# Three stacked blocks instead of four in the differential scores, and new durations and order tables for the plan

## The chip, the cores and the metric

The kernel runs on one core of a Trainium2 chip. The metric is the device time of one execution in microseconds. Engines are named as in the profile: PE is TensorE (PEld its weight loads), DVE is VectorE, ACT is ScalarE, POOL is GpSimd, SP is SyncE, which here issues all the DMAs.

## The reference

Two layers of a diffusion block work on 512 image tokens and 256 context tokens, each of width 1024. In a layer one wide product makes the inputs of four mixers (a state space scan, differential attention, grouped-query attention, latent attention), their outputs go through `w_out`, and a squared-ReLU feed-forward part of width 4096 follows. In the last layer the context gives keys and values only. Everything is float32. The mixer that the change touches is this one, with four heads, score dimension 32 and value dimension 64:

```python
def differential_attention(q1, q2, k1, k2, v, lam, scale):
    p = attn_probs(q1, k1, scale) - lam * attn_probs(q2, k2, scale)
    return jnp.einsum('bkgqt,bktd->bkgqd', p.astype(v.dtype), v)
```

So each head takes two softmaxes, each over scores that contract 32 values.

## The kernel before

**Tiling.** Tokens lie along the free axis: a tile has 128 feature rows and up to 768 tokens (512 image, 256 context). Large products run on TensorE in its fast float32 format (fp32r). For precision each operand is split into a high and a low part, and three products are summed: high by high, high by low, low by high. The feed-forward part of a layer is nothing but such products; they carry the name `p` in the profile.

**Stages.** The span goes through: start-up with the modulation vectors and the first projections; the mixers of layer 0 up to about 450 us; its output projection and feed-forward part up to about 1035 us; the seam of the layers and the mixers of layer 1 up to about 1395 us; its output projection and feed-forward part; the final norm.

**The differential scores.** `diff_prep` (line 1164) applies the rotary embedding to a tile of queries or keys (four score vectors of 32 rows), splits it into a high tile and a low tile (`hldq`, `hldk`, ending in h and l), and builds four stacks from them, one for each of the two heads hh and the two softmaxes m. A stack is a tile of 128 rows: four blocks of 32 rows, each copied out of the high or the low tile by a DMA of its own from SBUF to SBUF, issued on SP's queue (`stack`, line 1160). The key stack `sdk` holds high, high, low, low, the query stack `sdq` high, low, high, low. One matmul that contracts the 128 rows thus sums all four products. `diff_attn` (line 1251) calls `scores` (line 1182) on these stacks; the result is `d_s` in the profile (512 and 256 columns for image queries). DVE takes its maximum (`d_m`), ACT the exponential (`d_p`), TensorE transposes the mix of the two softmaxes (`d_t`) and multiplies by the values (`d_o`), and DVE or ACT stores (`yo`). Two such pairs of heads, j = 0 and 1, are worked on in each of the two layers. The latent attention contracts 96 rows in three separate matmuls instead (`m_s`).

**The order of the work.** No engine takes its work in the order of the program text. Each call through `nc` is recorded as an operation of a `Plan` (class at line 168), and at the end `order` (line 387) plays a model of the five queues: an operation gets a duration from `cost` (line 322), a `late` time that its result needs on top, and a `HOP` between engines; SP's operations also occupy a DMA model with 330 GB/s. Where several operations of an engine could start, the one with the lowest rank goes first: its number in the program text plus an entry of the table `BIAS`, looked up by stage, engine and tile name; EARLY brings forward those that read PSUM. A second table, `ASK`, shifts the rank in which tiles of one kind get their buffers. Neighbouring matmuls on one output are one operation up to a duration of `GROUP`. The order that comes out is written into the five instruction lists, and each engine works through its list strictly in that order: an instruction that waits holds up everything behind it. All of this happens when the program is built; on the chip the plan has no instruction. Because every call is issued in one place, every instruction has line 474 in the profile, and tiles have to be told by name.

The entry of the cost function for a DMA was one line, whatever its two ends:

```python
        self.bytes = 4 * (x.box[1] - x.box[0]) * x.width()
        return 0.45, 1.4
```

and a DVE operation that the model starts while POOL is still busy (`pool > s`) was lengthened by `0.3 * min(cost, pool - s)`.

Of the kernel before, what the change touches and what calls it, by code (L numbers as in the profile page):

```python
# [13 lines left out]
F32R = mybir.dt.float32r  # L14
# [153 lines left out]
class Plan:  # L168
# [3 lines left out]
    HOP = 0.2  # L172
# [4 lines left out]
        (0, 'ACT', 'an'): -300, (0, 'ACT', 'cden'): 90, (0, 'ACT', 'ls'): -50, (0, 'ACT', 'n__q'): 570, (0, 'ACT', 'sq_'): -185, (0, 'ACT', 'wdks'):  # L177
        335, (0, 'ACT', 'wdqs'): -510, (0, 'ACT', 'xn_h'): -350, (0, 'DVE', 'an'): -50, (0, 'DVE', 'cden'): 125, (0, 'DVE', 'dg'): -140, (0, 'DVE',
        'ds'): -285, (0, 'DVE', 'gq'): -190, (0, 'DVE', 'gs_'): 295, (0, 'DVE', 'lpr'): 55, (0, 'DVE', 'ls'): -50, (0, 'DVE', 'modT'): -300, (0,
        'DVE', 'n__q'): -70, (0, 'DVE', 'n__r'): -120, (0, 'DVE', 'n__t'): 185, (0, 'DVE', 'neg'): 270, (0, 'DVE', 'sel'): -165, (0, 'DVE', 'sil'):  # L180
        340, (0, 'DVE', 'sq_'): 125, (0, 'PE', 'n__ms'): 210, (0, 'PE', 'pdk'): 180, (0, 'PE', 'pdq'): 300, (0, 'PE', 'pdv'): -5, (0, 'PE', 'pm'):
        -100, (0, 'PE', 'pn'): -5, (0, 'POOL', 'epsT'): 260, (0, 'POOL', 'heads'): -310, (0, 'POOL', 'tri'): -630, (0, 'POOL', 'wdks'): 390, (0,
        'POOL', 'wdqs'): -120, (0, 'SP', 'h_'): -5, (0, 'SP', 'par'): -15, (0, 'SP', 'rope'): -5, (0, 'SP', 'wdq_'): 245, (1, 'ACT', 'cd_'): 300, (1,
        'ACT', 'ckv'): 65, (1, 'ACT', 'cq'): 50, (1, 'ACT', 'cqh_h'): -315, (1, 'ACT', 'cqn_s'): 735, (1, 'ACT', 'cqx'): -180, (1, 'ACT', 'cvb'): 540,
# [8 lines left out]
        -440, (1, 'ACT', 'tdv'): -300, (1, 'ACT', 'tgvv'): 395, (1, 'ACT', 'wckvs'): -15, (1, 'ACT', 'wcqs'): -20, (1, 'ACT', 'wcqxs'): -70, (1,
        'ACT', 'wdvs'): 70, (1, 'ACT', 'wgas'): 710, (1, 'ACT', 'wgbs'): -275, (1, 'ACT', 'wgks'): -250, (1, 'ACT', 'wgvvs'): 5, (1, 'ACT', 'wks'):
        -290, (1, 'ACT', 'wst'): -600, (1, 'ACT', 'wus_'): 15, (1, 'ACT', 'wxss'): -120, (1, 'ACT', 'wzs'): 15, (1, 'ACT', 'yg_'): -635, (1, 'ACT',
        'yn_q'): 5, (1, 'ACT', 'yn_r'): 150, (1, 'ACT', 'yn_s'): -370, (1, 'ACT', 'ztz_'): -80, (1, 'DVE', 'acs'): -400, (1, 'DVE', 'btm'): -250, (1,
        'DVE', 'cd_'): -460, (1, 'DVE', 'ckv'): -705, (1, 'DVE', 'cq'): -135, (1, 'DVE', 'cqh_l'): -25, (1, 'DVE', 'cqn_q'): -440, (1, 'DVE',
        'cqn_r'): 615, (1, 'DVE', 'cqx'): -135, (1, 'DVE', 'cvb'): -650, (1, 'DVE', 'cvc'): -120, (1, 'DVE', 'cvxs'): -170, (1, 'DVE', 'd_____m'): 75,
# [23 lines left out]
        (2, 'ACT', 'acc_'): 275, (2, 'ACT', 'n___q'): -1015, (2, 'ACT', 'n___r'): 70, (2, 'ACT', 'r___'): -370, (2, 'ACT', 'sq___'): -255, (2, 'ACT',  # L222
# [99 lines left out]
    def cost(self, eng, name, args, kw, out):  # L322
# [3 lines left out]
        if eng == "PE":  # L326
# [1666 lines left out]
```

## Time and profile before

| | |
|---|---|
| time, three runs | 1800.88, 1803.46, 1809.90 us; median 1803.46 us |
| time of the profiled execution | 1804.01 us |
| its span, first to last instruction | 1802.3 us |
| mean granted TensorE clock | 0.985 of full speed |
| DMA issues | stack copies `sdk`, `sdq` of 96 or 64 KB, beside 256 KB weight tiles |

The profile shows one execution. Busy times are sums over an engine's instructions; an idle time is put down to what released the instruction after it. A row of a timeline gives start, duration, engine, operation, output tile and inputs, and how many neighbouring instructions it stands for; in square brackets is the idle time before it and what ended it. SPq is the queue of SP. The recorded duration of a matmul includes its way through the array, so neighbouring ones overlap.

### The profile page before, as it was taken

The page shows a single profiled execution, that of the slowest core. Times are in us where ns is not written, and L with a number is a line of the kernel's source. Part 1 is how long each engine was busy: PE and PEld are TensorE (multiplying, and loading weights), DVE is VectorE, ACT ScalarE, POOL GpSimd, SP SyncE. Part 2 cuts the span into 40 slices and gives each one's busy share as a digit, 9 for nine tenths or more (in the row PEclk, how much of TensorE's full clock was granted, in tenths as well). Part 3 has the DMA queues.
Part 4 walks back from the last instruction along what each step waited for, and adds up shares of the span by engine and source line. Part 5 has one row for each costly group of instructions (what it writes and reads, how often), then busy time and mean ns, then how long its engine had stood idle before and what let it go on. Part 6 is the DMA issues. An engine that isn't in the chain of part 4 may idle for free.

```text
span 1802.3 us, 30217 instructions
## 1 busy us (share of the span) xinstructions
PE 1736.5 (96%) x11246; PEld 1460.8 (81%) x11246; DVE 1099.7 (61%) x2092; ACT 880.8 (49%) x1791; POOL 473.8 (26%) x441
## 2 busy tenths in 40 slices
PE   7999999999999999999999998999899999999996
PEld 4777887678889888888888877787678998888886
DVE  5567868876576764534534286696987863333335
ACT  4356778777455123123123455676877752323243
POOL 2412341210334001001003773244311320101066
PEclk9989999989999999999999999999999999999999
DMA  9475422132454532532433434414015553233234
GB/s 350 118 196 145 125 77 70 47 108 85 141 157 141 164 129 94 160 111 93 162 112 99 146 103 114 104 46 112 20 41 165 175 172 94 94 95 97 95 114 127
DMA packets 116755, 216.29 MB, mean 120 GB/s; under 512 B 15360, under 2 KB 22528, under 8 KB 116608
## 3 DMA queue, kind: packets, MB, share of 16 engines
q1 hardware_dynamic: 116608, 214.36, 38.7%
q8 instruction: 89, 1.46, 0.3%
q14 instruction: 58, 0.48, 0.1%
HBM read 185.99 MB, written 8.13 MB: 108 GB/s over the span
## 4 chain that ended last, share of the span: by engine, by line
PE 82%; DVE 5%; DMA 3%; issue 3%; POOL 2%; ACT 2%; SPq 2%; DVEq 0%; POOLq 0%; ACTq 0%
PE p L474 47%; PE po L474 3%; PE pr L474 2%; PE m_s L474 2%; SPq L474 2%; PE pxs L474 2%; PE pz L474 2%; PE d_s L474 1%; PE m_o L474 1%; PE m_t L474 1%; PE d_o L474 1%; PE g_s L474 1%; PE g_o L474 1%; PE pe L474 1%; PE d_t L474 1%
## 5 line engine op out<-in xcount | busy, mean ns | idle before, releaser
L474 ACT ACTIVATE w_0s<-w 128x512 fp32r<-128x512 f32 x256 | 161.0, 629 | 383.4 <-PE p L474 364.0
L474 POOL TENSOR_TENSOR r<-r 128x512 f32<-128x512 f32 (+2 forms) x80 | 89.4, 1118 | 622.9 <-ACT a_0h L474 382.9
L474 DVE TENSOR_TENSOR w_0s<-w,w_0s 128x512 fp32r<-128x512 f32 x216 | 150.6, 698 | 166.0 <-ACT w_0s L474 165.7
L474 DVE SCALAR_TENSOR_TENSOR h<-p,modT,h 128x512 f32<-128x512 f32 (+1 forms) x104 | 63.0, 625 | 140.6 <-PE p L474 140.5
L474 DVE SCALAR_TENSOR_TENSOR junk<-mv,cb 128x512 bf16<-128x512 f32 x128 | 93.6, 741 | 66.5 <-DMA mv<-in_modw_dram 66.2
L474 ACT ACTIVATE r<-p 128x512 f32<-128x512 f32 (+2 forms) x80 | 47.9, 598 | 169.4 <-PE p L474 169.2
L474 DVE TENSOR_REDUCE d_m<-d_s 128x1 f32<-128x768 f32 (+1 forms) x80 | 66.9, 846 | 42.9 <-PE d_s L474 42.6
L474 ACT ACTIVATE d_p<-d_s,d_m 128x768 f32<-128x768 f32 (+1 forms) x80 | 65.0, 814 | 26.3 <-DVE d_m L474 18.3
L474 POOL TENSOR_TENSOR w_0s<-w,w_0s 128x512 fp32r<-128x512 f32 x40 | 53.7, 1352 | 47.5 <-ACT w_0s L474 41.4
L474 POOL TENSOR_TENSOR acc<-acc,sq 128x256 f32<-128x256 f32 (+1 forms) x48 | 50.9, 1061 | 39.3 <-ACT sq L474 29.6
L474 PE MATMUL p<-xm_0h,w_0s 128*128 128x512 f32 (+1 forms) x176 | 54.2, 354 | 0.1
L474 PE MATMUL p<-xm_3h,w_0s 128*128 128x512 f32 (+1 forms) x176 | 54.1, 353 | 0.0
L474 PE MATMUL p<-xm_1h,w_0s 128*128 128x512 f32 (+1 forms) x176 | 54.0, 353 | 0.0
L474 PE MATMUL p<-xm_7h,w_0s 128*128 128x512 f32 (+1 forms) x176 | 54.0, 354 | 0.0
L474 PE MATMUL p<-a_5h,w_0s 128*128 128x512 f32 (+1 forms) x176 | 54.0, 353 | 0.0
L474 PE MATMUL p<-a_2h,w_0s 128*128 128x512 f32 (+1 forms) x176 | 54.0, 353 | 0.0
L474 PE MATMUL p<-a_0h,w_0s 128*128 128x512 f32 (+1 forms) x176 | 54.0, 353 | 0.0
L474 PE MATMUL p<-a_4h,w_0s 128*128 128x512 f32 (+1 forms) x176 | 54.0, 353 | 0.0
L474 PE MATMUL p<-a_3h,w_0s 128*128 128x512 f32 (+1 forms) x176 | 53.9, 352 | 0.0
L474 PE MATMUL p<-xm_6h,w_0s 128*128 128x512 f32 (+1 forms) x176 | 53.9, 353 | 0.0
L474 PE MATMUL p<-a_6h,w_0s 128*128 128x512 f32 (+1 forms) x176 | 53.9, 352 | 0.0
L474 PE MATMUL p<-xm_4h,w_0s 128*128 128x512 f32 (+1 forms) x176 | 53.9, 352 | 0.0
(2515 smaller groups left out, 5614.1 us busy)
## 6 DMA issues: line engine op xcount, KB each, us to landing
w<-in_w_dram SPq DMA_DIRECT2D x320, 256.0 KB, 2.6
mv<-in_modw_dram SPq DMA_DIRECT2D x96, 256.0 KB, 2.7
mk<-in_modk_dram SPq DMA_DIRECT2D x64, 256.0 KB, 3.7
wr<-in_wout_dram SPq DMA_DIRECT2D x32, 256.0 KB, 3.0
h<-in_xT_dram SPq DMA_DIRECT2D x16, 384.0 KB, 6.3
mw<-in_mod_dram SPq DMA_DIRECT2D x16, 384.0 KB, 6.7
wo<-in_wout_dram SPq DMA_DIRECT2D x32, 192.0 KB, 2.4
y<-yd SPq DMA_DIRECT2D x6, 384.0 KB, 3.4
```

The lines of the kernel that those rows point to most:

```text
L474: i = fn(*[x.real() if isinstance(x, View) else x for x in args], **{k: x.real() if isinstance(x, View) else x for k, x in kw.items()}).ins
```

## The change

It has three parts. The stacks get three blocks, high by high, high by low and low by high, and the score matmul contracts rows 0 to 95; the product of the two low parts is no longer in the sum. The functions `cost`, `take` and `order` get other durations, among them a longer one for copies from SBUF to SBUF with twice the bytes, a fixed 0.1 us (TURN) for an operation of plain float32 matmuls, a shorter hop with a `late` time for ACT, DVE and POOL, and another charge for DVE beside POOL. And every entry of `BIAS` and `ASK` is another (some entries are new, some are gone), so that the order on all queues is another. DRAM tiles are marked as such, which lets the cost function tell the copies.

```diff
-    HOP = 0.2
+    HOP, NEXT = 0.04, 0.1
+    TURN = 0.1
...
         if eng == "PE":
             if name == "transpose":
-                return 0.109, 0.2
+                return 0.083, 0.19
             w = args[1]
             if w.dt == F32R:
-                return max(0.12, 0.454 * n), 0.17
+                return max(0.118, 0.452 * n), 0.13
...
         if eng == "ACT":
-            return 0.17 + 0.85 * n + 0.27 * extra, 0.0
+            return 0.1 + 0.83 * n + 0.05 * extra, 0.1 + 0.05 * extra
         if eng == "DVE":
             if name == "tensor_reduce":
-                return 0.15 + 1.04e-3 * kw["in_"].width(), 0.0
+                return 0.07 + 1.05e-3 * kw["in_"].width(), 0.08
...
-            return 0.14 + 1.12 * n, 0.0
+            return 0.07 + 1.06 * n, 0.08
         if eng == "POOL":
-            return 0.4 + 1.75 * n, 0.0
+            return (0.1 + 0.6 * n, 0.1) if name in ("memset", "affine_select") else (0.3 + 1.8 * n, 0.05)
         x = out if isinstance(out, View) else args[1] if len(args) > 1 else kw["in_"]
         self.bytes = 4 * (x.box[1] - x.box[0]) * x.width()
+        if isinstance(out, View) and any(isinstance(y, View) and y.t.space is None for y in ins) and out.t.space is None:
+            self.bytes *= 2
+            return 0.6, 1.4
         return 0.45, 1.4
...
             if e == "POOL":
                 pool = s + cost
-            elif e == "DVE" and pool > s:
-                cost += 0.3 * min(cost, pool - s)
+            elif e == "DVE" and pool > s and not op.psum:
+                cost += 0.55 * min(1.1, pool - s)
...
-                    stack(s, hl, 2 * hh + m, (0, 0, 1, 1) if which == "dk" else (0, 1, 0, 1), n)
+                    stack(s, hl, 2 * hh + m, (0, 0, 1) if which == "dk" else (0, 1, 0), n)
...
-                a, b = [scores(f"d{l}_{j}_{t}_{hh}_{m}", [(dst["dq", j, hh, m], dst["dk", j, hh, m])], t) for m in range(2)]
+                a, b = [scores(f"d{l}_{j}_{t}_{hh}_{m}", [(dst["dq", j, hh, m][0:96], dst["dk", j, hh, m][0:96])], t) for m in range(2)]
```

## Rows read from the trace of the kernel before

**Rows 1.** The page: span, and busy time of the engines with shares and instructions.

```profile
span 1802.3 us, 30217 instructions
...
PE 1736.5 (96%) x11246; PEld 1460.8 (81%) x11246; DVE 1099.7 (61%) x2092; ACT 880.8 (49%) x1791; POOL 473.8 (26%) x441
```

**Rows 2.** Busy time by stretch: length, busy per engine (instructions), granted clock, DMA share, GB/s.

```profile
450.00:1035.00 585.00, 585.00 (x3423) 508.21 (x3422) 299.62 (x600) 185.87 (x314) 131.90 (x102) 1.00 0.42 132
1035.00:1170.00 135.00, 120.97 (x750) 102.69 (x749) 95.81 (x145) 75.33 (x154) 62.23 (x44) 0.96 0.40 107
...
1395.00:1755.00 360.00, 358.33 (x1913) 306.88 (x1913) 165.69 (x268) 148.47 (x283) 71.08 (x70) 1.00 0.38 117
```

**Rows 3.** TensorE's waits: tile, releaser; us in total, times, longest.

```profile
PE d_s L474 <- DMA sdk<-hldk_0l: 5.4, 1, 5.4
PE d_s L474 <- DMA sdq<-hldq_0l: 3.8, 1, 3.8
...
PE pk L474 <- DMA mk<-in_modk_dram: 3.3, 3, 2.6
PE d_s L474 <- ACT d_p L474: 3.1, 1, 3.1
...
PE d_t L474 <- DVE yo L474: 2.6, 1, 2.6
...
PE m_s L474 <- DMA mk_0h<-krh0h: 2.0, 1, 2.0
```

**Rows 4.** Busy time in six stretches at half clock between 45 and 1300 us.

```profile
90.30:97.10 6.80, 5.68 (x17) 4.75 (x17) 2.61 (x4) 1.59 (x3) 0.00 (x0) 0.50 0.86 204
...
124.50:131.30 6.80, 6.33 (x40) 5.46 (x33) 3.04 (x6) 0.63 (x1) 1.04 (x1) 0.50 0.99 336
...
370.20:380.40 10.20, 9.38 (x37) 6.67 (x37) 3.98 (x7) 3.18 (x8) 1.65 (x2) 0.50 0.24 54
...
1093.90:1100.70 6.80, 3.62 (x11) 3.04 (x12) 2.01 (x4) 1.48 (x3) 0.28 (x1) 0.50 0.74 205
...
1158.70:1162.10 3.40, 3.40 (x19) 2.67 (x19) 2.52 (x6) 2.51 (x8) 0.00 (x0) 0.50 0.16 59
...
1220.20:1223.60 3.40, 3.40 (x26) 2.48 (x25) 1.07 (x5) 0.24 (x1) 1.61 (x6) 0.51 0.65 151
```

**Rows 5.** Timeline of TensorE around the first differential scores of layer 0.

```profile
87.17 0.40 PE L474 MATMUL pdv<-xn_4h,wdv10s 128*128 128x512 f32 x1
91.42 0.98 PE L474 MATMUL d_s<-sdk,sdq 128*128 128x512 f32 x2 [3.85 <-DMA sdq<-hldq_0l]
92.19 0.63 PE L474 MATMUL pdv<-xn_5h,wdv10s 128*128 128x512 f32 x1
```

**Rows 6.** Timeline of SP's queue before the first differential scores of both layers.

```profile
75.61 5.79 SPq L474 DMA_DIRECT2D sdk<-hldk_0h  x8
81.50 5.69 SPq L474 DMA_DIRECT2D sdk<-hldk_0l  x8
...
89.15 0.58 SPq L474 DMA_DIRECT2D sdq<-hldq_0l  x1
...
1085.50 3.68 SPq L474 DMA_DIRECT2D sdq<-hldq_0l  x6
...
1093.70 1.14 SPq L474 DMA_DIRECT2D sdk<-hldk_0l  x2
```

**Rows 7.** Groups of TensorE by shape: count, busy us, mean ns, idle before.

```profile
L474 PE MATMUL d_s<-sdk,sdq 128*128 128x512 f32 x64 | 28.5, 446 | 13.0 <-DMA sdk<-hldk_0l 5.4 <-DMA sdq<-hldq_0l 3.8 <-ACT d_p L474 3.1
...
L474 PE MATMUL m_s<-mk_0h,mq_0h 96*128 96x512 f32 x8 | 4.2, 523 | 2.0 <-DMA mk_0h<-krh0h 2.0
...
L474 PE MATMUL m_s<-mk_3l,mq_3h 96*128 96x512 f32 x8 | 3.2, 396 | 0.0
```

**Rows 8.** Timeline of DVE before yo at 1218 us, and of DVE and POOL at 1769 us.

```profile
1211.64 1.77 DVE L474 TENSOR_TENSOR ga<-ga,r 128x512 f32<-128x512 f32 x1
...
1768.56 5.01 POOL L474 TENSOR_TENSOR w_256s<-w,w_256s 128x512 fp32r<-128x512 f32 x4
...
1768.97 4.89 DVE L474 TENSOR_TENSOR acc<-acc,sq 128x256 f32<-128x256 f32 x1
```

More of the change, by code (lines that the diff above doesn't have):

```diff
@@ L176 @@
     BIAS = {
[L177 to L184, printed above, removed]
@@ L193 @@
[L193 to L196, printed above, removed]
@@ L216 @@
-        'wcqxs'): -30, (1, 'POOL', 'wcs'): -145, (1, 'POOL', 'wdqs'): 130, (1, 'POOL', 'wdvs'): 390, (1, 'POOL', 'wgas'): -640, (1, 'POOL', 'wgks'):
-        -200, (1, 'POOL', 'wgvvs'): -300, (1, 'POOL', 'wxss'): 300, (1, 'POOL', 'wzs'): 475, (1, 'SP', 'gks__'): 125, (1, 'SP', 'gqs_'): 960, (1,
[4 rows of a table removed]
-        (2, 'ACT', 'acc_'): 275, (2, 'ACT', 'n___q'): -1015, (2, 'ACT', 'n___r'): 70, (2, 'ACT', 'r___'): -370, (2, 'ACT', 'sq___'): -255, (2, 'ACT',
-        'w___s'): -120, (2, 'ACT', 'wr_s'): -295, (2, 'ACT', 'xm_h'): 410, (2, 'ACT', 'xn_h'): 235, (2, 'DVE', 'a__l'): -50, (2, 'DVE', 'acc_'): 540,
@@ L224 @@
-        (2, 'DVE', 'gs_'): 235, (2, 'DVE', 'h_'): -25, (2, 'DVE', 'junk_'): -195, (2, 'DVE', 'modT'): 30, (2, 'DVE', 'n___q'): -80, (2, 'DVE',
-        'n___r'): -305, (2, 'DVE', 'w___s'): -105, (2, 'DVE', 'wr_s'): -835, (2, 'DVE', 'xm_l'): -520, (2, 'DVE', 'xn_l'): -405, (2, 'PE', 'n___ms'):
-        -350, (2, 'PE', 'p___'): 25, (2, 'PE', 'pcb'): -195, (2, 'PE', 'pk'): 50, (2, 'PE', 'pl'): 60, (2, 'PE', 'pq_'): -435, (2, 'PE', 'pr_'): 100,
-        (2, 'POOL', 'acc_'): -140, (2, 'POOL', 'r___'): 100, (2, 'POOL', 'w___s'): -280, (2, 'POOL', 'wq_s'): -20, (2, 'SP', 'mk_'): -325, (2, 'SP',
@@ L260 @@
-        -615, (3, 'POOL', 'wzs'): -305, (3, 'POOL', 'xw_'): -15, (3, 'SP', 'gks__'): 120, (3, 'SP', 'gqs_'): -20, (3, 'SP', 'h_'): 415, (3, 'SP',
[3 rows of a table removed]
-        (3, 'SP', 'wu_'): 50, (3, 'SP', 'wxs_'): -5, (3, 'SP', 'y_'): -120, (4, 'ACT', 'a__h'): 480, (4, 'ACT', 'n___q'): -315, (4, 'ACT', 'n___r'):
-        -560, (4, 'ACT', 'nf_q'): 50, (4, 'ACT', 'nf_r'): -180, (4, 'ACT', 'r___'): 20, (4, 'ACT', 'sq___'): 325, (4, 'ACT', 'w___s'): 70, (4, 'ACT',
-        'wq_s'): 50, (4, 'ACT', 'wr_s'): 290, (4, 'DVE', 'a__l'): -230, (4, 'DVE', 'acc_'): -515, (4, 'DVE', 'h_'): -180, (4, 'DVE', 'n___q'): 340,
@@ L267 @@
-        (4, 'DVE', 'n___r'): -120, (4, 'DVE', 'n___t'): -280, (4, 'DVE', 'w___s'): 710, (4, 'DVE', 'wr_s'): 290, (4, 'PE', 'nf_ms'): -15, (4, 'PE',
-        'p___'): 105, (4, 'PE', 'pq_'): -180, (4, 'PE', 'pr_'): 910, (4, 'POOL', 'acc_'): 70, (4, 'POOL', 'r___'): -205, (4, 'POOL', 'w___s'): 10, (4,
-        'POOL', 'wq_s'): -295, (4, 'SP', 'out'): -250, (4, 'SP', 'w____'): -320, (4, 'SP', 'wr__'): 10
+        (0, 'ACT', 'ls'): 120, (0, 'ACT', 'ms'): -790, (0, 'ACT', 'n__q'): -300, (0, 'ACT', 'n__r'): -75, (0, 'ACT', 'sq_'): -95, (0, 'ACT', 'wdks'):
@@ new lines @@
+        -305, (0, 'ACT', 'wdqs'): 115, (0, 'ACT', 'xn_h'): -265, (0, 'DVE', 'an'): 490, (0, 'DVE', 'cden'): -510, (0, 'DVE', 'dg'): -5, (0, 'DVE',
+        'ds'): 300, (0, 'DVE', 'lpr'): -70, (0, 'DVE', 'ls'): 55, (0, 'DVE', 'modT'): 255, (0, 'DVE', 'n__q'): 70, (0, 'DVE', 'n__r'): 270, (0, 'DVE',
+        'n__t'): 475, (0, 'DVE', 'neg'): -105, (0, 'DVE', 'nlam'): -95, (0, 'DVE', 'sq_'): 300, (0, 'PE', 'n__ms'): 65, (0, 'PE', 'pdk'): -20, (0,
+        'PE', 'pdq'): 80, (0, 'PE', 'pdv'): 275, (0, 'PE', 'pn'): -175, (0, 'POOL', 'ones'): 50, (0, 'POOL', 'sil'): 305, (0, 'POOL', 'tri'): -670,
@@ new lines @@
+        (0, 'POOL', 'wdks'): -20, (0, 'POOL', 'wdqs'): -40, (0, 'POOL', 'wdvs'): -5, (0, 'SP', 'h_'): -30, (0, 'SP', 'par'): -425, (0, 'SP', 'rope'):
+        105, (0, 'SP', 'wdq_'): -180, (0, 'SP', 'wdv_'): 140, (1, 'ACT', 'ckv'): 190, (1, 'ACT', 'cq'): -220, (1, 'ACT', 'cqn_q'): 45, (1, 'ACT',
+        'cvb'): 75, (1, 'ACT', 'cvc'): 580, (1, 'ACT', 'cvxs'): 285, (1, 'ACT', 'd_____p'): -435, (1, 'ACT', 'd_____pt'): 5, (1, 'ACT', 'dec'): -70,
+        (1, 'ACT', 'dk'): 25, (1, 'ACT', 'dn__q'): 285, (1, 'ACT', 'dq'): -120, (1, 'ACT', 'dr_'): 420, (1, 'ACT', 'dsq_'): 170, (1, 'ACT', 'dte'):
@@ new lines @@
+        'wdqs'): -30, (1, 'ACT', 'wdvs'): 275, (1, 'ACT', 'wgas'): 150, (1, 'ACT', 'wgbs'): 85, (1, 'ACT', 'wgks'): 380, (1, 'ACT', 'wgvvs'): -350,
+        (1, 'ACT', 'wks'): 5, (1, 'ACT', 'wo_s'): -10, (1, 'ACT', 'wst'): 70, (1, 'ACT', 'wus_'): -100, (1, 'ACT', 'wxss'): 5, (1, 'ACT', 'wzs'): -30,
+        (1, 'ACT', 'xtm_'): -460, (1, 'ACT', 'yg_'): -150, (1, 'ACT', 'ym_'): -485, (1, 'ACT', 'yn_q'): -625, (1, 'ACT', 'yn_r'): 25, (1, 'ACT',
+        'yn_s'): -235, (1, 'ACT', 'ys_h'): 300, (1, 'ACT', 'ztz_'): -115, (1, 'DVE', 'cd_'): 20, (1, 'DVE', 'ckv'): -15, (1, 'DVE', 'cq'): -605, (1,
@@ new lines @@
+        'DVE', 'cqn_q'): -300, (1, 'DVE', 'cqn_r'): 310, (1, 'DVE', 'cqx'): 50, (1, 'DVE', 'cvb'): -255, (1, 'DVE', 'cvc'): 170, (1, 'DVE', 'cvxs'):
+        5, (1, 'DVE', 'd_____m'): 355, (1, 'DVE', 'd_____p'): -550, (1, 'DVE', 'da'): -120, (1, 'DVE', 'dn__q'): -310, (1, 'DVE', 'dr_'): -25, (1,
+        'DVE', 'ee__'): -5, (1, 'DVE', 'g____m'): -320, (1, 'DVE', 'gb'): -25, (1, 'DVE', 'gkn_q'): 140, (1, 'DVE', 'gkn_r'): 360, (1, 'DVE',
+        'gqn_q'): -90, (1, 'DVE', 'gs_'): -265, (1, 'DVE', 'h_'): 190, (1, 'DVE', 'hldk_l'): 285, (1, 'DVE', 'hlgkl'): -20, (1, 'DVE', 'hlgq_l'):
@@ new lines @@
+        (1, 'POOL', 'rddq_'): 5, (1, 'POOL', 'rk'): -105, (1, 'POOL', 'rq'): -470, (1, 'POOL', 'wbs'): 5, (1, 'POOL', 'wckvs'): -420, (1, 'POOL',
+        'wcqs'): -455, (1, 'POOL', 'wcqxs'): 440, (1, 'POOL', 'wcs'): -80, (1, 'POOL', 'wdqs'): -905, (1, 'POOL', 'wdvs'): -540, (1, 'POOL', 'wgas'):
+        -400, (1, 'POOL', 'wgbs'): 675, (1, 'POOL', 'wgks'): -415, (1, 'POOL', 'wgvvs'): -5, (1, 'POOL', 'wxss'): 5, (1, 'POOL', 'wzs'): 50, (1,
[5 rows of a table added]
+        'acc_'): 180, (2, 'ACT', 'cb'): -360, (2, 'ACT', 'n___r'): -50, (2, 'ACT', 'sq___'): 125, (2, 'ACT', 'w___s'): 115, (2, 'ACT', 'wq_s'): 175,
@@ new lines @@
+        (2, 'ACT', 'wr_s'): 260, (2, 'DVE', 'a__l'): -180, (2, 'DVE', 'acc_'): 460, (2, 'DVE', 'gs_'): -355, (2, 'DVE', 'h_'): -235, (2, 'DVE',
+        'junk_'): 50, (2, 'DVE', 'modT'): 440, (2, 'DVE', 'n___q'): 45, (2, 'DVE', 'n___r'): -245, (2, 'DVE', 'w___s'): 280, (2, 'DVE', 'wr_s'): -320,
+        (2, 'DVE', 'xm_l'): 165, (2, 'DVE', 'xn_l'): 120, (2, 'PE', 'n___ms'): -20, (2, 'PE', 'pcb'): -130, (2, 'PE', 'pk'): 110, (2, 'PE', 'pq_'):
+        20, (2, 'PE', 'pr_'): 315, (2, 'POOL', 'acc_'): 575, (2, 'POOL', 'r___'): 175, (2, 'POOL', 'w___s'): -20, (2, 'SP', 'mk_'): 380, (2, 'SP',
@@ new lines @@
+        'ACT', 'wgbs'): 370, (3, 'ACT', 'wks'): -70, (3, 'ACT', 'wo_s'): -210, (3, 'ACT', 'wst'): -655, (3, 'ACT', 'wus_'): -5, (3, 'ACT', 'wxss'):
+        105, (3, 'ACT', 'wzs'): 420, (3, 'ACT', 'xn_h'): 305, (3, 'ACT', 'xtm_'): 20, (3, 'ACT', 'yg_'): -300, (3, 'ACT', 'ym_'): -10, (3, 'ACT',
+        'yn_q'): -50, (3, 'ACT', 'yn_r'): 350, (3, 'ACT', 'yn_s'): 405, (3, 'ACT', 'ys_h'): -50, (3, 'DVE', 'acs'): 1065, (3, 'DVE', 'btm'): 285, (3,
+        'DVE', 'cd_'): -235, (3, 'DVE', 'ckv'): -475, (3, 'DVE', 'cq'): 120, (3, 'DVE', 'cqh_l'): -95, (3, 'DVE', 'cqn_q'): 305, (3, 'DVE', 'cqn_r'):
@@ new lines @@
+        'wks'): -55, (3, 'DVE', 'wo_s'): 310, (3, 'DVE', 'wst'): -120, (3, 'DVE', 'wus_'): -120, (3, 'DVE', 'xn_l'): 355, (3, 'DVE', 'yn_q'): 1070,
+        (3, 'DVE', 'yn_r'): -300, (3, 'DVE', 'yo_'): 415, (3, 'DVE', 'ys_l'): -5, (3, 'DVE', 'ztz_'): -5, (3, 'PE', 'cqn_ms'): 405, (3, 'PE',
+        'd_____o'): -35, (3, 'PE', 'd_____s'): -445, (3, 'PE', 'd_____t'): -50, (3, 'PE', 'dn__ms'): -5, (3, 'PE', 'g____o'): -300, (3, 'PE',
+        'g____s'): 95, (3, 'PE', 'g____t'): 10, (3, 'PE', 'gkn_ms'): 40, (3, 'PE', 'gqn_ms'): -700, (3, 'PE', 'kvn_ms'): 645, (3, 'PE', 'm____o'):
@@ new lines @@
+        120, (3, 'POOL', 'wgks'): 480, (3, 'POOL', 'wgvvs'): -305, (3, 'POOL', 'wxss'): -120, (3, 'POOL', 'wzs'): -120, (3, 'SP', 'gks__'): -115, (3,
[4 rows of a table added]
+        'a__h'): -30, (4, 'ACT', 'n___r'): -275, (4, 'ACT', 'nf_q'): -70, (4, 'ACT', 'sq___'): -55, (4, 'ACT', 'w___s'): 20, (4, 'ACT', 'wq_s'): 120,
+        (4, 'ACT', 'wr_s'): -155, (4, 'ACT', 'xm_h'): -430, (4, 'DVE', 'a__l'): 35, (4, 'DVE', 'acc_'): 510, (4, 'DVE', 'h_'): -340, (4, 'DVE',
+        'n___q'): -45, (4, 'DVE', 'n___t'): -325, (4, 'DVE', 'nf_r'): -60, (4, 'DVE', 'w___s'): -15, (4, 'DVE', 'wr_s'): -55, (4, 'DVE', 'xm_l'): 10,
@@ L270 @@
+        (4, 'PE', 'n___ms'): -125, (4, 'PE', 'nf_ms'): 290, (4, 'PE', 'p___'): 345, (4, 'PE', 'pq_'): -170, (4, 'POOL', 'acc_'): 85, (4, 'POOL',
+        'r___'): 30, (4, 'POOL', 'w___s'): 5, (4, 'POOL', 'wq_s'): 255, (4, 'SP', 'w____'): -90, (4, 'SP', 'wq__'): 370, (4, 'SP', 'wr__'): -160
     }
     ASK = {
-        (0, 'cden'): 180, (0, 'epsT'): 300, (0, 'gq'): -340, (0, 'gs_'): -50, (0, 'h_'): -325, (0, 'heads'): -440, (0, 'ident'): 80, (0, 'lpr'): 5,
-        (0, 'ls'): -345, (0, 'modT'): -50, (0, 'ms'): 790, (0, 'mw__'): -395, (0, 'n__ms'): -55, (0, 'neg'): -675, (0, 'nlam'): -15, (0, 'ones'): 765,
@@ L311 @@
-        'wq_s'): 15, (4, 'wr__'): 20, (4, 'xm_h'): 5, (4, 'xm_l'): 5
+        (0, 'an'): -300, (0, 'cden'): 50, (0, 'dg'): 5, (0, 'ds'): 55, (0, 'epsT'): -455, (0, 'heads'): -115, (0, 'ident'): -75, (0, 'lpr'): -95, (0,
+        'ls'): -75, (0, 'modT'): 350, (0, 'ms'): -280, (0, 'n__ms'): 5, (0, 'n__t'): 5, (0, 'neg'): 275, (0, 'nlam'): -400, (0, 'ones'): -230, (0,
+        'par'): 300, (0, 'pdk'): -20, (0, 'pdq'): -100, (0, 'pm'): -5, (0, 'pn'): -5, (0, 'rope'): 20, (0, 'sel'): 120, (0, 'sil'): -565, (0, 'sq_'):
@@ L360, in take @@
         op = self.ops[-1] if self.ops else None
-        if not (eng == "PE" and op is not None and op.eng == "PE" and op.out is out.t and op.cost + cost <= self.GROUP):
+        if not (eng == "PE" and op is not None and op.eng == "PE" and op.out is out.t and op.cost - op.turn + cost <= self.GROUP):
             op = Op(len(self.ops), eng)
@@ L365, in take @@
             op.bytes = self.bytes if eng == "SP" else 0
+            op.turn = op.cost = self.TURN if eng == "PE" and (name == "transpose" or args[1].dt != F32R) else 0.0
             self.ops.append(op)
@@ L391, in order @@
             op.rank = op.n + self.BIAS.get(op.kind, 0)
-            if op.eng not in ("PE", "SP") and any(t.space == PSUM for t in op.tiles):
+            op.psum = any(t.space == PSUM for t in op.tiles)
+            if op.eng not in ("PE", "SP") and op.psum:
                 op.rank -= self.EARLY
@@ L408, in arrive @@
         def arrive(op):
-            op.at = max((o.end if o.eng == op.eng == "PE" else o.end + (o.late + (0.03 if o.eng == op.eng else self.HOP))
+            op.at = max((o.end if o.eng == op.eng == "PE" else o.end + (o.late + (self.NEXT if o.eng == op.eng else self.HOP))
                          for o in op.before), default=0.0)
```

187 lines of the change are left out of this document (89 added, 98 removed), and 19 rows, old and new, of the table BIAS.

## The prediction

> **What bounds the kernel now.** I read the page's busy shares first, then the busy time by stage, then TensorE's waits, then the granted clock around the longest of them, then the queues behind those waits. TensorE is busy for 1736.5 of the 1802.3 us of the span and no other engine passes 61% [rows 1]. In the two feed-forward stages it never stops: 585.00 of 585.00 us between 450 and 1035 us, and 358.33 of 360.00 us between 1395 and 1755 us [rows 2]. More than half the span can therefore gain nothing from another order of the same matmuls. What is open lies in the mixers and at the seam of the layers: 14.0 us idle in 1035 to 1170 alone [rows 2].
>
> That idle time is a few long stalls, not many short ones. Six of them make 20 us: the first differential scores of layer 0 wait 3.8 us and those of layer 1 5.4 us for a stack copy, the modulation matmuls pk wait 3.3 us for weights (in three waits), a d_s waits 3.1 us for ACT, a d_t 2.6 us for DVE's yo, and the first latent scores m_s 2.0 us for a key copy [rows 3]. Each is paid twice. Behind each the granted clock stands at half (0.50 or 0.51 of full speed, the 1.2 GHz level) for 3.4 to 10.2 us, and TensorE is busy 5.68, 6.33, 9.38, 3.62, 3.40 and 3.40 us in those stretches [rows 4]. At full clock half of that would have done, so the six dips cost 31.81 / 2 = 15.9 us. Stalls and dips together: 20.2 + 15.9 = 36 us, 6.0 us for one stall with its dip.
>
> They happen because every engine works its list in the order that the plan wrote down. From 87.17 to 91.42 us TensorE did nothing, although the rest of the pdv product it was in the middle of lay ready: it stood behind the d_s in the list, and came right after it, at 92.19 us [rows 5]. The plan had put the d_s too early, since it took the copies before it for shorter than they are.
>
> **The change, part by part.** All sums are against the profiled execution: span 1802.3 us, its own time 1804.0 us, which is 0.5 us above the median of the three runs shown; I take that 0.5 us off at the end.
>
> *Three blocks for four.* A stack takes one copy of 32 rows per block, on SP's queue. There are 2 layers x 2 pairs x 2 kinds x 4 stacks = 32 stacks, so 128 copies become 96 and nothing is added. The issue of eight takes 5.79 and 5.69 us in layer 0 (0.72 us each), of six 3.68 us in layer 1 (0.61 us each) [rows 6]. Most of the 32 lie beside TensorE's work and their removal is worth nothing there; the two places where they count are the first scores of each layer.
> In layer 0, the sixteen key copies are issued in a row from 75.61 us, then the query copies; the fourth of these, issued at 89.15 us, releases the d_s [rows 6]. With three blocks, four of the key copies that bring low parts go (4 x 0.71 = 2.8 us) and one query copy (0.6 us): the d_s can start 3.4 us earlier. Its stall falls from 3.8 to 0.4 us, and with so short a stall I count the dip as gone too (5.68 / 2 = 2.8 us). Together 6.2 us.
> In layer 1 the low copies are issued from 1085.50 us, and the low key copies that release the d_s from 1093.70 us [rows 6]. Four low query copies go (4 x 0.61 = 2.4 us) and one low key copy (0.6 us): 3.0 us. The stall falls from 5.4 to 2.4 us, about as long as the 2.6 us before yo, which had a dip behind it [rows 3, 4], so this dip stays. Together 3.0 us.
> Sum of this part with the order left as it is: 9.2 us. If other work stands in the gap anyway, it is nothing.
>
> *96 rows for 128 in the d_s matmuls.* The trace has no d_s with 96 rows, but the latent scores have them. A d_s of 512 columns is recorded with 446 ns; m_s of 96 rows and 512 columns with 523 ns for the first head and with 396 ns for the last [rows 7]. Over 144 d_s matmuls this bounds the effect at +77 x 144 = +11 us and -50 x 144 = -7 us. I take zero: the first m_s is long because it stands behind a stall at half clock, and the last one is within 50 ns of the d_s although it has a quarter fewer rows, so the columns set the duration. That the scores lose the product of the two low parts costs no time.
>
> *The planner's durations.* They run when the program is built and add no instruction; they matter through the order alone. What they say now against the trace: a copy from SBUF to SBUF is charged 0.6 us of SP's time instead of 0.45, and twice its bytes. The trace has 0.57 to 0.72 us per copy [rows 6], so sixteen were planned up to 16 x 0.27 = 4.3 us too short, which is the size of the stalls of 3.8 and 5.4 us. DVE beside a POOL instruction is charged up to 0.55 x 1.1 = 0.605 us more, where before it was at most 30% of its cost. For the DVE tensor_tensor of 512 columns that makes 0.07 + 1.06 x 0.512 + 0.605 = 1.22 us instead of 0.93 us; the trace has 1.77 us beside POOL [rows 8], and a chain of four like that ends in the yo that the d_t waits 2.6 us for. Both moves go in the right direction, the first all the way and the second a third of it. The hop between engines falls from 0.2 to 0.04 us, with up to 0.1 us moved into each producer: for 512 columns a consumer is now planned 0.14 us sooner after ACT (0.525 + 0.14 for 0.605 + 0.2) and 0.18 us sooner after DVE (0.613 + 0.12 for 0.713 + 0.2). No row here prices a hop alone, so I give it no term and keep its risk for the rival below.
>
> *The two order tables.* Every instruction may move on every queue, DMAs on SP's too, so the trace of before can only bound this. What can be had from the order beyond the 9.2 us: the latent copy 2.0 + 9.38 / 2 = 6.7 us; what is left in layer 1, 2.4 + 3.62 / 2 = 4.2 us; pk 3.3 + 6.33 / 2 = 6.5 us; the d_s behind ACT 3.1 + 1.7 = 4.8 us; yo 2.6 + 1.7 = 4.3 us. Sum 26.5 us. The other end is that as many new stalls arise as old ones go, or more, at 6.0 us each: four more would be +24 us. Of the 26.5 us, 17.4 us (latent, layer 1, pk) hang on DMAs, two of the three on exactly the copies whose charge is mended, so I take a little over a third as the net gain: 9.5 us. It is nearer to the lower end than to the middle, because new places mean new mistakes.
>
> Sum: 1804.0 - 9.2 - 9.5 = 1785.3, less 0.5 for the median: 1785 us, 1.0% faster.
>
> **The rivals.**
> *Nearly all stalls go.* For it: each of the six is a wait for something planned too short, while ready work stood behind it. Against it: the charge for DVE beside POOL is still 0.5 us short of the rows. 1804 - 9.2 - 26.5 = 1768 us.
> *Stall for stall.* The new order fills the old gaps and opens as many others, and then the removed copies are hidden as well, since the d_s no longer wait for them. For it: the six stalls arose under a plan that held them to be free. What is left is a part of the first term, some 3 us: 1801 us, no change that can be told.
> *Slower: DVE behind a row of POOL instructions.* The plan now sets consumers 0.14 to 0.18 us closer, and its extra charge for DVE ends at 0.605 us. At 1768.97 us DVE's acc took 4.89 us while POOL ran four instructions in a row for 5.01 us [rows 8]; the plan charges 0.6 us of that. Whatever is queued behind such a DVE instruction, and the matmuls listed for its result, come 4 us late, and TensorE pays 6.0 us with the dip. It makes the kernel slower as soon as there are two more such stalls than now (9.2 / 6.0 = 1.5); four more give 1804 - 9.2 + 24 = 1819 us. Against it: the old charge was smaller still, and of the six stalls only the yo is of this kind.
> The Trainium skill says the same of this pair in "SBUF — State Buffer", section "Who interferes with whom": a DVE instruction with two SBUF inputs and a GpSimd instruction that reads SBUF exclude each other for the whole instruction, and the loser blocks. The 4.89 us agrees; by that rule the new charge, which is capped, is wrong wherever POOL has several such instructions in a row, and the time would go towards this rival's 1819 us.
>
> **How the numbers follow.** Forecast, around 1785 us with an own range of 1776 to 1796: 0.46. Nearly all stalls go, 1768: 0.14. Stall for stall, 1801: 0.22. Slower, from 1808 up: 0.18. The range takes in the first three and the near edge of the last: 1766 to 1810 us; the ends of the 96-row matmul (+11, -7) fit inside it around the forecast. About 0.5% (9 us) is what a measurement of this kernel can tell from no change. Faster by more than that, under 1794 us: 0.42 of the forecast's 0.46, all of the 0.14 and 0.02 of the third, 0.58. Within it: 0.04 + 0.20 and 0.01 of the fourth, 0.25. Slower: 0.17.
>
> **What would show it.** TensorE's waits on the copies sdk, sdq and mk_0h should sum to under 4 us instead of 11.2, and the stretches at half clock between 45 and 1300 us should be four or fewer instead of six. The feed-forward stages should keep their length within 2 us. The d_s of 512 columns with 96 rows should be recorded with 420 to 460 ns. SP should issue 96 stack copies. The prediction is wrong in its first term if the first d_s of each layer stalls as long as before, and in its second if the waits on DVE and ACT grow by what the waits on DMAs lose.

## The result and the profile after

The changed kernel takes 1786.24 us (median of four runs, 1785.69 to 1787.5), the kernel before 1804.73 us beside it (four runs, 1800.88 to 1809.9). The ratio is 0.9897, with a 95% interval of 0.987 to 0.9923: faster by 1.0%. The forecast was 1785 us. The sum was right, but its two terms were not, as the experiments show.

The page of the kernel after, with the span and the busy time of each engine, answers to [rows 1]:

```profile
span 1784.2 us, 30207 instructions
...
PE 1733.0 (97%) x11246; PEld 1455.8 (82%) x11246; DVE 1073.5 (60%) x2092; ACT 878.9 (49%) x1791; POOL 480.3 (27%) x441
```

TensorE's idle time (span less busy) fell from 65.8 to 51.2 us; its matmuls are as many as before, and their busy time is only 3.5 us less, although only one stretch at half clock is left between 45 and 1300 us where there were six (see below). The profiled execution took 1785.9 us, 18.1 us less than that of before. The busy time by stretch of the kernel after, in the columns of [rows 2]; the last two stretches are the one around the first differential scores and the one at half clock:

```profile
450.00:1035.00 585.00, 583.16 (x3432) 505.95 (x3431) 299.53 (x597) 186.82 (x314) 139.00 (x106) 1.00 0.41 132
1035.00:1170.00 135.00, 128.20 (x778) 105.80 (x777) 107.27 (x171) 85.24 (x174) 60.35 (x42) 0.99 0.35 94
1395.00:1755.00 360.00, 357.94 (x1916) 306.76 (x1915) 155.40 (x249) 145.97 (x274) 80.59 (x77) 1.00 0.37 116
90.30:97.10 6.80, 4.94 (x35) 3.88 (x36) 2.83 (x6) 2.00 (x5) 0.00 (x0) 1.00 0.67 165
...
1056.96:1060.37 3.41, 3.32 (x8) 2.65 (x9) 2.50 (x4) 1.31 (x3) 1.16 (x1) 0.54 0.58 166
```

Between 45 and 1300 us the stretch at 1057 is the only one left at half clock, where there were six [rows 4]. TensorE's waits after (tile, releaser; us in total, times, longest):

```profile
PE nf_ms L482 <- DVE acc L482: 4.4, 2, 2.4
PE pdk L482 <- POOL sil L482: 4.2, 1, 4.2
PE pdk L482 <- ACT xn_0h L482: 2.6, 1, 2.6
PE n_ms L482 <- DVE sq L482: 2.5, 2, 2.2
PE d_s L482 <- DMA sdk<-hldk_0h: 2.1, 1, 2.1
PE m_t L482 <- ACT ym L482: 1.8, 1, 1.8
PE p L482 <- DVE h L482: 1.7, 1, 1.7
...
PE d_s L482 <- ACT d_p L482: 1.3, 2, 0.8
```

Of the six long stalls of [rows 3] one is left, the 2.1 us of the first differential scores of layer 0. The timeline of SP's queue before those scores, after (start, us of issue, tile, count); it answers to [rows 6]:

```profile
79.79 4.71 SPq L482 DMA_DIRECT2D sdq<-hldq_0h  x7
84.59 1.35 SPq L482 DMA_DIRECT2D sdq<-hldq_0l  x2
86.04 1.02 SPq L482 DMA_DIRECT2D mk<-in_modk_dram  x2
87.11 1.15 SPq L482 DMA_DIRECT2D sdk<-hldk_0h  x2
88.30 0.59 SPq L482 DMA_DIRECT2D sdk<-hldk_0l  x1
```

The first d_s starts at 92.16 us, 0.7 us later than before [rows 5]; the last at 1178.8, 20.7 us earlier (1199.5 before). So the gain lies behind the first scores of layer 0, not ahead of them.

### The profile page after: what moved, and what is told of

Same layout as the page of the kernel before. It is cut to its first block, busy times and chain, and to the rows that moved or that the text cites. A ratio compares the mean times of both kernels' runs of the same rounds, so it can differ in the third digit from the quotient of the medians.

```text
span 1784.2 us, 30207 instructions
## 1 busy us (share of the span) xinstructions
PE 1733.0 (97%) x11246; PEld 1455.8 (82%) x11246; DVE 1073.5 (60%) x2092; ACT 878.9 (49%) x1791; POOL 480.3 (27%) x441
## 5 line engine op out<-in xcount | busy, mean ns | idle before, releaser
L482 DVE SCALAR_TENSOR_TENSOR junk<-mv,cb 128x512 bf16<-128x512 f32 x128 | 90.8, 719 | 97.3 <-DMA mv<-in_modw_dram 97.1
L482 DVE SCALAR_TENSOR_TENSOR n_t<-h,gs,n_r 128x512 f32<-128x512 f32 (+1 forms) x64 | 51.5, 824 | 4.5 <-POOL acc L482 3.5
L482 PE MATMUL p<-a_7h,w_0s 128*128 128x512 f32 (+1 forms) x176 | 54.0, 353 | 0.0
L482 PE MATMUL p<-a_1h,w_0s 128*128 128x512 f32 (+1 forms) x176 | 54.0, 353 | 0.0
L482 PE MATMUL p<-xm_5h,w_0s 128*128 128x512 f32 (+1 forms) x176 | 53.9, 353 | 0.0
```

Of the source, the lines that this page charges most:

```text
L482: i = fn(*[x.real() if isinstance(x, View) else x for x in args], **{k: x.real() if isinstance(x, View) else x for k, x in kw.items()}).ins
```

## The experiments

Each was timed beside the kernel before on the same chip, and the ratios are to that. "Before's order" means that every queue keeps the exact order of the kernel before, so that only what is named changes.

**1. Three blocks, before's order.** The fourth copy of every stack is dropped when the list is written out, and the d_s read 96 rows:

```diff
+                if getattr(op, "drop", False):
+                    continue
...
+                nc.ops[-1].drop = b == 3
...
+                        nc.ops[-1].calls[-1] = fn, (args[0], args[1][0:96], args[2][0:96]), kw
```

> The kernel before, with every instruction of every queue in its old order, but the fourth copy of each stack left out (96 copies instead of 128) and the scores contracted over rows 0 to 95 (the product of the low parts is not summed, as in the changed kernel). If the first term of the prediction is right: 9.2 us faster than before (ratio 0.995): the first d_s of layer 0 starts 3.4 us earlier, its stall falls from 3.8 to about 0.4 us and the stretch at half clock behind it is gone, the stall of layer 1 falls from 5.4 to about 2.4 us and keeps its dip. If the copies are hidden anyway: ratio 0.999 to 1.001, with the stalls at other instructions.

Measured: 1788.53 against 1802.39 us, ratio 0.9909 (0.989 to 0.9928): 16.4 us by the ratio, 13.9 by the medians, where the prediction gave this part 9.2 us. Without any new order the kernel is nearly at the time of the changed one. The waits of this kernel, in the columns as above:

```profile
PE d_t L476 <- DVE yo L476: 2.6, 1, 2.6
PE d_s L476 <- DMA sdk<-hldk_0h: 2.5, 1, 2.5
...
PE m_s L476 <- DMA mk_0h<-krh0h: 1.9, 1, 1.9
...
PE d_s L476 <- DMA sdq<-hldq_0h: 0.8, 1, 0.8
```

Two stalls went that the prediction had left to the order: pk behind its weights (3.3 us) and d_s behind ACT (3.1 us) [rows 3]. The timelines of SP's queue around the weights that pk waits for show why, first before, then in this kernel:

```profile
120.26 0.59 SPq L474 DMA_DIRECT2D sdq<-hldq_1l  x1
120.95 1.02 SPq L474 DMA_DIRECT2D mk<-in_modk_dram  x2
```

```profile
111.24 0.59 SPq L476 DMA_DIRECT2D sdq<-hldq_1h  x1
111.93 1.02 SPq L476 DMA_DIRECT2D mk<-in_modk_dram  x2
```

The weights mk for pk stand on the same queue behind the copies of the second pair, and leave 9.0 us sooner. The d_s behind ACT is the same in layer 1, one step further off: before, ACT stood in front of a weight, and so the d_p after it came late. Timelines of before (SP, ACT, TensorE), and SP of this kernel:

```profile
1150.66 1.14 SPq L474 DMA_DIRECT2D sdk<-hldk_1l  x2
1151.89 0.53 SPq L474 DMA_DIRECT2D wxs<-in_win_dram  x1
...
1155.22 0.63 ACT L474 ACTIVATE wxs11s<-wxs 128x512 fp32r<-128x512 f32 x1 [5.03 <-DMA wxs<-in_win_dram]
...
1157.97 0.61 PE L474 MATMUL d_s<-sdk,sdq 128*128 128x512 f32 x2 [3.11 <-ACT d_p L474]
```

```profile
1136.19 0.51 SPq L476 DMA_DIRECT2D sdk<-hldk_1l  x1
1136.79 0.53 SPq L476 DMA_DIRECT2D wxs<-in_win_dram  x1
```

The releaser that the wait names is ACT; what was late is a weight behind stack copies on SP. The account closes on the profiled executions: stalls 15.6 us before (3.8 + 5.4 + 3.3 + 3.1) and 3.9 us now (2.5 + 0.8 and 0.6 behind an issue), and the half-clock stretches cost (16.85 + 3.23 + 3.40) / 2 = 11.7 us for 15.9: 11.7 + 4.2 = 15.9 us, against 15.6 us by the spans. The one term against it is the stretch behind the latent scores, which became longer; busy time in this kernel:

```profile
361.80:378.80 17.00, 16.85 (x68) 11.99 (x68) 7.43 (x13) 5.89 (x13) 3.71 (x3) 0.50 0.16 47
```

**2. 96 rows alone.** Before's order with all 128 copies; only the last line of the diff above.

> The kernel before in its old order with all 128 copies, and only the d_s matmuls cut to rows 0 to 95 (the product of the low parts is not summed). If the columns alone set a matmul's duration: ratio 0.999 to 1.001 and a recorded 440 to 455 ns for 512 columns. By the bounds of the prediction: up to +11 us (ratio 1.006) or -7 us (0.996).

Measured: ratio 1.000 (0.9988 to 1.0012), and 450 ns recorded for a d_s of 512 columns. The rows cost and save nothing that can be told. So the whole of experiment 1 is the copies.

**3. Four blocks in the new order.** The changed kernel with the fourth copy put back, right behind the other copy from the same low tile, and the d_s over 128 rows:

```diff
+                if b == at:
...
+                    nc.ops[-1].calls.append((fn, (f(d[96:128, 0:n]), f(hl[1][32 * r : 32 * r + 32, 0:n])), kw))
```

> The changed kernel with every instruction in its new order, but the fourth copy of each stack put back (issued right behind the other copy out of the low tile) and the scores over 128 rows. If the copies are worth the first term in the new order too: 9 us slower than the changed kernel (ratio to before 0.995). If the new order hides them: within 2 us of the changed kernel (0.990). I expect something between, 3 to 6 us, since the changed kernel's first d_s of layer 0 still waits 2.1 us for a stack copy, and five more copies before it are 3.3 us.

Measured: 1800.64 us, ratio 0.9986 (0.9972 to 0.9999). The 32 copies cost 0.9986 - 0.9897 = 0.9 points, 16 us, in the new order too, and the order with its durations, alone, gives 2.5 us (0.2 to 5). Its waits:

```profile
PE d_s L482 <- DMA sdq<-hldq_0l: 5.1, 2, 3.1
...
PE d_t L482 <- ACT d_pt L482: 3.8, 1, 3.8
PE d_s L482 <- DMA sdk<-hldk_0l: 3.4, 1, 3.4
```

The new order has no more room for the copies than the old one had.

**4. Ready work ahead of the first scores.** Before with its four blocks; on TensorE alone, 4.5 us (layer 0) and 6 us (layer 1) of projection matmuls whose inputs lay ready are moved in front of the first d_s:

```diff
+            for op in moved:
+                out.remove(op)
+            out[at:at] = moved
```

> The kernel before with four blocks and its old order on DVE, ACT, POOL and SP; on TensorE alone, 4.5 us (layer 0) and 6 us (layer 1) of ready projection matmuls are taken ahead of the first d_s of each layer. If the stall is only a wrong place in the list: both stalls (3.8 and 5.4 us) and the dips behind them (2.8 and 1.8 us) go, 13.8 us faster (ratio 0.992). If the scores that come later cost the attention as much further on: ratio 0.998 to 1.001.

Measured: 1803.32 us, ratio 1.0009 (0.9993 to 1.0024): nothing. TensorE's timeline in this kernel:

```profile
93.97 0.51 PE L490 MATMUL d_s<-sdk,sdq 128*128 128x512 f32 x2
98.76 0.59 PE L490 MATMUL d_s<-sdk,sdq 128*128 128x512 f32 x2 [4.28 <-DMA sdq<-hldq_0h]
```

The first d_s has no stall any more, and the second has one of 4.28 us. The prediction read [rows 5] as a d_s placed too early. Moving work ahead of it does not help here, since its successors need the next stacks, and these come when SP has issued them; what was moved is what had stood between the first and the second d_s. In layer 1 the first scores wait 4.7 us in three places, for 5.4 us before. Whether still more ready work ahead of them would help was not tried.

**5 and 6. The copies of one pair alone.** As experiment 1, for head pair 0 or head pair 1 only. Pair 0 holds the stacks that the first scores of each layer wait for; pair 1 gates no first score.

```diff
+                nc.ops[-1].drop = b == 3 and d.t.args[3].split("_")[1] == "0"
```

> As e1 (old order, fourth copies and the product of the low parts left out), but for the first pair of heads (j = 0) of each layer only: 16 copies fewer. The prediction's first term holds that only these gate a first score: 9.2 us faster than before, all of it here. If instead SP's queue is what is short, so that every copy taken off it counts alike, about half of the 14 us that e1 gave: 5 to 9 us here and as much for the other pair.

> As e5, but for the second pair of heads (j = 1) only. By the prediction's first term: nothing (ratio 0.999 to 1.001), since these copies gate no first score. If the copies hold up the weights that stand behind them on SP's queue: the waits of pk on mk at 122 us and of d_s on ACT at 1155 us are gone or shorter, 4 to 9 us faster (0.995 to 0.998).

Measured: pair 0 1792.56 us, ratio 0.9949 (0.9933 to 0.9964); pair 1 1791.92 us, ratio 0.9946 (0.9927 to 0.9965). About half of the gain comes from copies that the prediction held to be free. The waits with pair 1 alone dropped, and then with pair 0 alone:

```profile
PE d_s L476 <- DMA sdk<-hldk_0l: 6.0, 1, 6.0
...
PE d_s L476 <- DMA sdq<-hldq_0l: 4.0, 1, 4.0
```

```profile
PE d_s L476 <- ACT d_p L476: 3.6, 1, 3.6
...
PE d_s L476 <- DMA sdk<-hldk_0h: 2.2, 1, 2.2
```

Without pair 1's copies the first scores stall as long as before, while the waits on mk and on ACT are gone. Without pair 0's it is the other way round: the first scores of layer 1 wait 2.2 us for 5.4, and pk (1.6 us) and the d_s behind ACT are still there. The two effects nearly add up: 0.51 and 0.54 points, and 0.91 for both together. One thing blurs the sizes: neither of these two profiled executions has a stretch at half clock behind the latent scores, where before has one that cost 9.38 / 2 = 4.7 us. That much of the gain of each profiled execution may not be the work of that pair's copies.

**7. The fourth copy with one column.** Before's order and 96 rows; all 128 copies are issued, but the 32 fourth ones move one column, which nothing reads.

```diff
+                if b == 3:
...
+                    nc.ops[-1].calls[-1] = fn, tuple(x[:, 0:1] for x in args), kw
```

> The kernel before in its old order, scores over 96 rows (without the product of the low parts), and all 128 copies issued, but the fourth of each stack copies one column of its 32 rows instead of 768 or 512. If the issue on SP's queue is the price of a copy: no gain, ratio 0.998 to 1.001, and the fourth copies still take 0.5 to 0.6 us of SP. If it is the bytes: as e1, 0.991.

Measured: 1802.52 us, ratio 1.0007 (0.9997 to 1.0017). All of the gain is gone although next to none of the bytes are back. The four stalls that experiment 1 removed or shortened are there again:

```profile
PE d_s L474 <- DMA sdk<-hldk_0l: 4.8, 1, 4.8
PE d_s L474 <- ACT d_p L474: 4.5, 1, 4.5
PE pk L474 <- DMA mk<-in_modk_dram: 4.3, 3, 3.7
...
PE d_s L474 <- DMA sdq<-hldq_0h: 3.3, 1, 3.3
```

SP's timeline in this kernel, where four of the eight low copies have one column:

```profile
82.66 5.82 SPq L474 DMA_DIRECT2D sdk<-hldk_0l  x8
```

Eight whole ones took 5.69 us [rows 6]. The price of a copy is its issue on SP, not what it moves. This is plainest for pk and for the weight in front of ACT's d_p, which read no stack and only stand behind the copies on the queue.

**8 to 11. Durations and tables.** 8: before (four blocks, its own tables) planned with the new durations. 9: after (three blocks, its own tables) planned with the old durations. 10 and 11: after with both tables empty, with the new and with the old durations.

```diff
-    BIAS = {
...
+    BIAS, ASK = {}, {}
```

> The kernel before with four blocks and its old tables, but planned with the new durations, so that the order on all queues is found anew. If durations nearer to the trace make a better order by themselves: faster than before, 0.992 to 0.998. If the tables belong to the durations they were found with: slower, 1.005 to 1.02.

> The changed kernel (three blocks, new tables) planned with the old durations. If the tables belong to the durations they were found with, as the opposite mix showed (+1.2%): slower than the changed kernel by 0.5 to 2%, ratio to before 0.995 to 1.010. If the tables carry the gain alone: 0.990.

> The changed kernel planned with its new durations, but with both tables empty, so that ranks are the order of the program text. The tables' worth: I expect 1 to 4% slower than the changed kernel (ratio to before 1.00 to 1.03).

> As e10, but with the old durations: the same three blocks and empty tables. If the new durations make the better plan where no table has been fitted to either: 0.3 to 1.5% slower than e10. If they matter only through the tables: within 0.3% of e10.

| tables and blocks | old durations | new durations |
| --- | --- | --- |
| of before, four blocks | 1 | 1.0117 (1.0104 to 1.0131) |
| of after, three blocks | 1.0068 (1.0051 to 1.0085) | 0.9897 (0.987 to 0.9923) |
| empty, three blocks | 1.0074 (1.005 to 1.0098) | 1.0035 (1.0023 to 1.0046) |

The new table helps only with the durations that it was found for: it gives 1.4 points with them and 0.1, which is none that can be told, with the others. For the old table there is only the upper row, which has four blocks and no empty table beside it. Where no table is fitted, the new durations are better by 0.4 points. Without its tables the changed kernel is slower than before, although it has three blocks.

**12. Key copies on ACT's queue.** The order of after; the 48 copies of the sdk stacks are issued by ACT instead of SP.

```diff
+                    if op.eng == "SP" and op.out and op.out.args[3].startswith(('sdk',)):
+                        fn = self.nc.scalar.dma_start
```

> The changed kernel in its order, but the 48 key copies (sdk) are issued on ACT's queue instead of SP's. If SP's issue time is what a copy costs: 4 to 10 us faster than the changed kernel (ratio to before 0.984 to 0.988), the waits on copies gone. If ACT, which has the exponentials of the same scores in its list, pays 0.6 us for each copy and holds them up: slower than the changed kernel by up to 10 us (0.991 to 0.995).

Measured: 1789.77 us, ratio 0.9919 (0.9904 to 0.9933), not faster than after (0.9897), and the intervals meet. Rows of this kernel (a group of copies by tile: shortest, median and longest ns, first and last start; then timelines of DVE and of ACT):

```profile
L484 ACTq DMA_DIRECT2D sdk<-hldk_0h x16: 514/602/845, 81.4 to 1091.1; - x16
...
91.95 0.96 DVE L484 TENSOR_REDUCE d_m<-d_s 128x1 f32<-128x768 f32 x1 [4.14 <-PE d_s L484]
...
92.29 1.65 ACTq L484 DMA_DIRECT2D sdk<-hldk_0l  x1
93.99 0.90 ACT L484 ACTIVATE d_p<-d_s,d_m 128x768 f32<-128x768 f32 x1 [5.24 <-DMA sdk<-hldk_0h]
```

An issue takes ACT as long as SP (median 602 ns here, 585 to 591 ns for the sdk copies of before on SP), and ACT's own work now stands behind copies: the maximum d_m is there at 92.91 us, and d_p starts 1.1 us later, when the copy in front of it has been issued. The rest of the 5.24 us is the wait for d_m itself. The place where work queues has moved, and nothing was won by it.

## Why the prediction was right or wrong

**The time: right, by two errors that cancel.** The copies gave 16 us instead of 9.2, tables and durations some 2 us instead of 9.5. The last is 0.9909 - 0.9897 = 0.1 points by experiment 1 (with both intervals, from 4 us lost to 8 us gained) and 0.14 by experiment 3 (0.2 to 5 us); both leave the 9.5 us out. That the sum came within 1.3 us of the measured time was luck.

**The step that failed** is the sentence "Most of the 32 lie beside TensorE's work and their removal is worth nothing there; the two places where they count are the first scores of each layer." It priced a copy only where a matmul waits for it. Experiment 7 shows that each takes its turn of 0.6 to 0.7 us on SP whatever its size, and experiments 1 and 6 that the next weights on that queue pay for it: pk's wait and the d_s behind ACT, which the prediction put down to the order (6.5 and 4.8 us of the 26.5), went with the copies. 9.2 + 6.5 + 4.8 = 20.5 us, less the 3.7 us by which the latent stretch grew ((16.85 - 9.38) / 2), is 16.8 us: the terms had nearly the right sizes and stood under the wrong cause.

**The stalls of the first scores.** That they hang on the number of copies was right. That the plan "had put the d_s too early" found no support: with ready work in front of it, the same stall came at the next d_s (experiment 4). Layer 1 came out as worked out: 2.5 us left of 5.4, 2.4 forecast. In layer 0 experiment 1 leaves 0.6 and 0.8 us, for 0.4 forecast. Its first d_s came 1.8 us earlier (89.63 for 91.42 us) and not 3.4, because in that execution SP also began the key copies 1.6 us later (77.23 for 75.61 us).

**Durations and tables.** Against experiment 1, the new order removed the latent stall and its long stretch (1.9 + 16.85 / 2 = 10.3 us) and the wait on yo (2.6 us). It gave most of it back, in several places. The first p matmul of layer 0 starts at 490.69 us, 8.8 us before that of experiment 1 (499.52), but the last one of the layer at 1047.54 for 1047.27: from the first to the last, this feed-forward part takes 556.8 us for 547.8. The new order has put 48 more pk matmuls in it, and TensorE, whose longest wait there was 0.7 us before, waits 1.7 us for DVE's h and 1.2 us for DVE's xm_3l. In the mixers of layer 1 there are new waits of 1.8 (m_t for ACT), 1.5, 1.3 and 1.2 us. The first pdq matmul of layer 1 started at 1053.16 us before, 1047.39 in experiment 1 and 1047.66 after: up to there the new order is worth nothing beside the copies, and from there to the end of the span it is worth 2.8 us (736.5 against 739.3 us). The larger part of the loss is in no wait. In experiment 1 TensorE's busy time fell by 4.5 us (1736.5 to 1732.0), about the 4.2 us that the stretches at half clock cost less. After, these cost 15.9 - 3.32 / 2 = 14.2 us less and the busy time fell by 3.5: by this reckoning some 11 us of busy time came in elsewhere, with as many matmuls. Where they lie was not found. I counted what the trace shows as lost in the old order as recoverable; it was what an order fitted to its own durations had left, and the new one leaves about as much elsewhere. For this term the rival of stall for stall was right.

**96 rows at nothing: right.** The ratio of experiment 2 says so, and the group of after by shape, which answers to [rows 7], has the same 446 ns:

```profile
L482 PE MATMUL d_s<-sdk,sdq 96*128 96x512 f32 x64 | 28.3, 446 | 4.5 <-DMA sdk<-hldk_0h 2.1 <-ACT d_p L482 1.3 <-issue 0.5
```

**The slower rival did not decide.** DVE's acc still stands beside POOL, 3.94 us for the 4.89 of [rows 8]; timeline of DVE after:

```profile
1754.60 3.94 DVE L482 TENSOR_TENSOR acc<-acc,sq 128x256 f32<-128x256 f32 x1 [2.01 <-POOL acc L482]
```

During it POOL ran three instructions in a row, and the other acc of this form, with POOL idle beside it, took 0.43 us. The Trainium skill's rule in "SBUF — State Buffer", section "Who interferes with whom", that a DVE instruction with two SBUF inputs contends with a GpSimd instruction that reads SBUF, agrees with these two rows. No new stall of that length came of it.

**The signs.** Waits on sdk, sdq and mk_0h: 2.1 us (under 4 forecast). Half-clock stretches: one (four or fewer). Stack copies: 96. The length of the feed-forward stages (within 2 us forecast) held in layer 1, 364.0 us from the first p matmul to the last for 364.9 before, and not in layer 0, 556.8 us for 547.8; the fixed windows shown above, with 583.16 of 585.00 us busy, don't show a length. The other signs came out, and none tells the two terms apart: I had named signs of the sum, where a sign for the split would have been whether the waits on mk and on ACT go without a new order.

**What stays open.** In experiment 1 the medians give 13.9 us and the ratio of the rounds 16.4; the single runs spread over 6 us. The two fastest of the six (1782.94 and 1784.42 us) had a mean granted clock of 0.994 and 0.993, the other four 0.989. An estimate: 17.0 us at half clock take 17.0 / 2 / 1787 = 0.005 off the mean, so the long stretch behind the latent scores was probably missing from these two, and without it the old order with three blocks is no slower than the new one. Only one of the six was profiled, so this is not shown. Whether fewer copies still, each of more rows, would gain more was not run.

## What to carry to other kernels

In these runs a DMA cost its turn on the queue that issues it, whether it moved one column, 96 KB or a 256 KB weight, and the one who paid was the next thing on that queue: price an added or removed DMA by what stands behind it, not only by who reads it. Follow a stall past the releaser that the profile names, through what that engine waited for, until a queue that is always busy; here one wait on ACT was a weight behind copies on SP. What a fitted order leaves idle isn't free to take: test it by making the change in the old order, and by putting the old work back in the new one.

## What the runs showed of the hardware

A copy of one column took as long to issue as one of the full width (eight with four of them short: 5.82 us, eight whole: 5.69 us), and a 256 KB weight no longer (0.53 us for wxs). ACT's queue took 0.52 to 0.60 us for a copy (medians by tile), SP's 0.59.

How long the clock stays at half does not follow from the stall ahead of it: 2.0 us before the latent scores were followed by 10.2 us at half [rows 3, 4], 1.9 us at the same place in experiment 1 by 17.0 us, 2.0 us there in experiment 6 (pair 1) by none (1.00 from 361.8 to 378.8 us), and 2.1 us before the first scores of after by none (1.00 from 90.3 to 97.1). In the first three TensorE runs the same instructions in the same order. The length of a stall alone therefore does not price what comes behind it, and a forecast that counts a stretch as gone or as staying by the stall's length, as mine did, has no support in these runs.
